# Four output tiles held back behind the last FoX scores, three products on the old weight buffers, and the loads around them moved

## The chip, the core and the metric

The kernel runs on one core of a Trainium2 chip. The metric is the device time of one execution in microseconds (us), as the median of several runs. A profiled execution has its own time, and inside it the span from the first to the last instruction that the profiler recorded. The engines are TensorE (PE in the profile, its weight loads PEld), VectorE (DVE), ScalarE (ACT), GpSimd (POOL) and SyncE (SP), which here only issues transfers: it takes them strictly in program order, and a transfer that waits for a semaphore holds back all that stand behind it.

## What is computed

One step of a decoder layer, for 512 prompt positions and for 8 samples of 8 new positions each (64 rows), 576 columns in all. The attention has a FoX group and a DSA group of 8 heads each; the output projection `w_out` joins them:

```
h = x + concat([fox, dsa]) @ w_out          # w_out rows 0..1023 belong to FoX
f, new_g = conv_ffn(rms_norm(h, g_ffn), prev_g, w_gate, w_up, conv_w, conv_b, w_down)
y = h + f

# FoX of a sample: 1024 cached keys (8 pages of 128) and 8 new ones, 8 heads
s = einsum('bqhd,bkhd->bhqk', q, k) * scale + c_q - c_k
o = einsum('bhqk,bkhd->bqhd', softmax(s), v)
```

## The kernel before

All matrix products are made in three passes of a value split into a high and a low part (high by high, high by low, low by high), with the output features on the partitions and the columns (tokens) along the free axis in two halves of 288 (`HALF`). A product of 1024 inputs by 128 outputs on one half is 24 matmuls, called a product here.

The program is written through a scheduling layer: helper functions record instructions, and the layer sets the order on each engine from its own estimate of when they can start. "Lanes" are generators that `gemm` steps after every second input tile through `pump`; the rate of a lane says how many of its steps one such call takes.

The place of the change is the end of the attention. The output projection has 16 tiles (o = 0 to 15) of 128 output features. Its half 0 is done first, while the samples' FoX attention runs in two lanes beside it: `sa` (scores) and `sb` (values). A sample reads its 8 key pages and 8 value pages (512 KB each) from the cache; TensorE turns the keys (L1413), ACT and DVE split them (L196, L199), TensorE makes the scores (L1434, L1435), DVE and ACT make the softmax (L751 to L782), TensorE turns the weights (L1462) and multiplies them with the values (L1477), and `turned` (L1492, L1494) puts the result into `osum[0]`.

- `w_out_a` makes tiles 5 to 15 (and the DSA rows of tiles 0 to 4 earlier), `w_out_late` (L1369) the FoX rows of tiles 0 to 4 on half 0, for which only prompt columns are needed. Their weights come through `load_w` (L147, buffers `wraw`, `wh`, `wl`) one tile ahead; their sums of squares collect in `ssum0`, which `inverse_rms` (L1524 to L1530) turns into `yn0` with a short chain of small DVE instructions, called the Newton chain here.
- Half 1 of the FoX rows needs the samples, so it comes last: `stage` loads the prompt columns from `odr` (L1297), `fill` and `fill_sample` split them into `gxs`, and a loop over the 16 tiles loads weights (`load_wo`, L1634, buffers `wr`, `wu`, `wl`), multiplies, adds to the rows of h that `load_h` (L1590) brought back, and stores them (L1721). All of these transfers stand in SP's one queue.
- `taps` (L1697, L1698) turns the convolution weights, which SP loads at L1618 and L1619. `half0` normalizes half 0 of h within the same loop.
- Then the gate, up and down products of the MLP follow and fill the rest of the span.

Buffers of later pools lie on memory of earlier ones: the tile `x12`, into which `load_h` brings half 1 of h for tiles 0 to 7, lies where the pool `sx` had, among others, `ob`, `ptile`, `sq0` and the scratch tiles `ms`, `n4_y`, `n4_t` of the Newton chain; `wr0` to `wr3` lie where the key tiles `kraw` were.

Of the kernel before, what the change touches and what calls it, by code (L numbers as in the profile page):

```python
# [49 lines left out]
NLATE = 5  # L50
CTS = (3, 4, 4, 4, 3, 3)
# [4 lines left out]
def tile_hymba_step(  # L56
# [1340 lines left out]

    def fox_scores(b, keep):
# [18 lines left out]
        for w in range(2):  # L1417
# [11 lines left out]
            for h in range(HA):  # L1429
# [5 lines left out]
                T.matmul(sps, qz[:, h * P:(h + 1) * P], kl, start=False, stop=h == 7)  # L1435
# [96 lines left out]
    lane("sa", 2.068)  # L1532
    lane("sb", 1.7)
# [6 lines left out]
    w_out_a(range(NLATE, KD))  # L1540
    for o in range(NLATE):
        w_out_late(o)
# [4 lines left out]
    gxs = fill(fslots, 0, stage(old_x, 0, HALF, TP))  # L1547
# [15 lines left out]
    wp_ctx.close()  # L1563
# [8 lines left out]
    x2_ctx, x2 = opened("x2")  # L1572
    wq_ctx, wq = opened("wq")
    fn_ctx, fn = opened("fn")
    wb_ctx, wb = opened("wb")
# [70 lines left out]

    def multiply(acc, rows, start):


        for k, (wh, wl, xh, xl) in enumerate(rows):  # L1650
            T.matmul(acc, wh, xh, start=start and k == 0, stop=False, skip_group_check=not start)  # L1651
            T.matmul(acc, wh, xl, start=False, stop=False, skip_group_check=not start)  # L1652
        for k, (wh, wl, xh, xl) in enumerate(rows):
            T.matmul(acc, wl, xh, start=False, stop=k == len(rows) - 1, skip_group_check=not start)  # L1654
# [564 lines left out]
```

## Time and profile before

| | us |
|---|---|
| median of 3 runs | 2797.47 |
| lowest and highest | 2793.05, 2798.58 |
| the profiled execution, its own time | 2795.66 |
| its span in the profile | 2793.9 |

The profiled execution is 1.81 us under the median; outside its span lie 1.8 us. In the rows further down, a time is counted from the start of the span. A row of the timeline gives the start, how long it took, engine, line, operation, operands and count, and in brackets how long the engine was idle before and what ended that. The matmuls of TensorE overlap, so that the cost of one is read from start to start, not from its own length.

### The profile page before, as it was taken

Reading aid. Unit: us, or ns where it says so; the run is one execution under the profiler, and the core shown is the slowest. Engines: PE = TensorE matmul, PEld = TensorE weight load, DVE = VectorE, ACT = ScalarE, POOL = GpSimd, SP = SyncE. Lnnn points to the kernel's source line nnn. Section 1 sums busy time; section 2 is a strip of 40 time slices with the busy share of each in tenths; the row PEclk is TensorE's granted clock in tenths of the full one; section 3 lists DMA queues with packets and bytes.
Section 4 is the critical chain, followed back from the end, with each engine's and each line's share of the span. In section 5 each row is a group of like instructions: output and inputs, shape, how many; then the busy total and the mean of one; then the engine's idle time right before and its main releaser. Section 6 shows DMA issues by size and latency. Waiting matters only on the chain.

```text
span 2793.9 us, 53435 instructions
## 1 busy us (share of the span) xinstructions
PE 2709.0 (97%) x20679; PEld 2619.4 (94%) x20679; DVE 2080.8 (74%) x3701; ACT 1346.4 (48%) x2395; POOL 535.5 (19%) x707
## 2 busy tenths in 40 slices
PE   8999999999998999979999999999999999999999
PEld 7998999999898988869999999999999999999999
DVE  6669689555646655547988888888888878888877
ACT  6446644654765444435555454555545543333332
POOL 1333243323554000000012221211111110000000
PEclk9999999999999999989999999999999999999999
DMA  7224343435646699868645554554444476446553
GB/s 212 69 72 108 92 121 90 114 100 160 183 125 216 218 326 308 304 224 241 168 146 159 161 167 150 160 155 135 148 135 145 142 265 218 146 163 210 189 166 111
DMA packets 506776, 469.48 MB, mean 168 GB/s; under 512 B 33360, under 2 KB 451794, under 8 KB 506010
## 3 DMA queue, kind: packets, MB, share of 16 engines
q1 hardware_dynamic: 479481, 363.88, 44.2%
q0 software_dynamic: 26032, 100.12, 9.8%
q8 instruction: 162, 2.65, 0.4%
q10 hardware_dynamic: 1008, 2.06, 0.2%
q14 instruction: 93, 0.75, 0.1%
HBM read 385.37 MB, written 80.36 MB: 167 GB/s over the span
## 4 chain that ended last, share of the span: by engine, by line
PE 61%; DMA 4%; DVE 2%; issue 2%; ACT 1%; SPq 0%; POOL 0%; ACTq 0%; DVEq 0%; POOLq 0%
PE pgemm L1651 10%; PE pgemm L1652 9%; PE pgemm L1654 9%; PE pone L1651 7%; PE pone L1652 7%; PE pone L1654 7%; PE pone L1413 2%; PE pgemm L173 2%; PE pgemm L171 2%; PE pgemm L172 2%; PE pout L1477 1%; PE pq L1434 1%; PE pq L1435 1%; DMA wr<-in_w_down_dram 1%; DVE wl L1644 1%
## 5 line engine op out<-in xcount | busy, mean ns | idle before, releaser
L171 PE MATMUL pgemm<-xh,wh 128*128 128x288 f32 (+1 forms) x1824 | 551.2, 304 | 8.5 <-DVE rawT L1355 3.7
L173 PE MATMUL pgemm<-xh,wl 128*128 128x288 f32 (+1 forms) x1824 | 548.1, 301 | 0.7 <-DVE wl L152 0.7
L172 PE MATMUL pgemm<-xl,wh 128*128 128x288 f32 (+1 forms) x1696 | 509.9, 301 | 3.6 <-DVE xl L300 3.6
L1639 ACT CAST wu<-wr 128x1024 fp32r<-128x1024 f32 (+1 forms) x287 | 292.0, 1019 | 407.5 <-PE pgemm L1652 192.0
L1644 DVE TENSOR_TENSOR wl<-wr,wu 128x1024 fp32r<-128x1024 f32 (+1 forms) x287 | 337.4, 1179 | 37.8 <-ACT wu L1639 33.2
L171 PEld LDWEIGHTS pgemm<-xh,wh 128*128 128x128 f32 (+1 forms) x1824 | 344.9, 189 | 15.1 <-DVE rawT L1355 4.0
L173 PEld LDWEIGHTS pgemm<-xh,wl 128*128 128x128 f32 (+1 forms) x1824 | 345.3, 189 | 5.1 <-DVE wl L152 1.0
L172 PEld LDWEIGHTS pgemm<-xl,wh 128*128 128x128 f32 (+1 forms) x1696 | 321.0, 189 | 7.8 <-DVE xl L300 4.8
L1639 ACT CAST wu<-x 128x1024 fp32r<-128x1024 f32 (+1 forms) x198 | 201.7, 1022 | 258.2 <-PE pgemm L1652 127.5
L1651 PE MATMUL pgemm<-hi,wu 128*128 128x288 f32 x1024 | 280.2, 298 | 4.0 <-DVE ht L2120 3.2
L1651 PE MATMUL pgemm<-xh,wu 128*128 128x288 f32 x992 | 273.0, 301 | 11.3 <-issue 6.7
L1644 DVE TENSOR_TENSOR wl<-x,wu 128x1024 fp32r<-128x1024 f32 (+1 forms) x198 | 233.5, 1183 | 13.1 <-ACT wu L1639 9.0
L1651 PE MATMUL pone<-xh,wu 128*128 128x288 f32 x880 | 240.6, 299 | 2.5 <-ACT wu L1639 2.5
L1652 PE MATMUL pone<-xl,wu 128*128 128x288 f32 x880 | 240.9, 297 | 0.0
L1652 PE MATMUL pgemm<-lo,wu 128*128 128x288 f32 x856 | 232.8, 296 | 0.0
L1652 PE MATMUL pgemm<-xl,wu 128*128 128x288 f32 x824 | 225.2, 297 | 0.0
L1651 PEld LDWEIGHTS pgemm<-xh,wu 128*128 128x128 f32 x992 | 188.1, 190 | 14.9 <-issue 7.6
L1651 PEld LDWEIGHTS pgemm<-hi,wu 128*128 128x128 f32 x1024 | 193.6, 189 | 4.7 <-DVE ht L2120 3.8
L151 ACT CAST wh<-wraw 128x1024 fp32r<-128x1024 f32 (+1 forms) x122 | 127.3, 1045 | 113.6 <-PE pgemm L172 94.5
L152 POOL TENSOR_TENSOR wl<-wraw,wh 128x1024 fp32r<-128x1024 f32 (+1 forms) x51 | 122.0, 2392 | 287.5 <-ACT wh L151 279.2
L1799 POOL DMA_DIRECT2D opd<-pp x140 | 75.7, 542 | 525.8 <-DVE pp L199 501.7
L1651 PEld LDWEIGHTS pone<-xh,wu 128*128 128x128 f32 x880 | 166.5, 190 | 2.6 <-ACT wu L1639 2.6
(556 smaller groups left out, 6639.7 us busy)
## 6 DMA issues: line engine op xcount, KB each, us to landing
wraw<-in_w_in_dram SPq DMA_DIRECT2D x88, 512.0 KB
wr<-in_w_gate_dram SPq DMA_DIRECT2D x85, 512.0 KB
opd<-pp POOLq DMA_DIRECT2D x140, 288.0 KB, 4.0
wr<-in_w_up_dram SPq DMA_DIRECT2D x69, 512.0 KB
kraw<-in_cache_fox_k_dram SPq DMA_DIRECT2D x64, 512.0 KB
vraw<-in_cache_fox_v_dram SPq DMA_DIRECT2D x62, 512.0 KB
wr<-in_w_down_dram SPq DMA_DIRECT2D x38, 512.0 KB
wraw<-in_w_out_dram SPq DMA_DIRECT2D x32, 512.0 KB
```

Source lines behind the costliest of these rows:

```text
L151: A.copy(h[:, :k, :m], raw[:, :k, :m])
L152: (G if share[0] and not u else V).tensor_sub(l[:, :k, :m], raw[:, :k, :m], f(h)[:, :k, :m])
L171: T.matmul(acc[:m, :], h[:, j, :m], xh[:, c], start=kt == 0, stop=False)
L172: T.matmul(acc[:m, :], h[:, j, :m], xl[:, c], start=False, stop=False)
L173: T.matmul(acc[:m, :], l[:, j, :m], xh[:, c], start=False, stop=kt == nk - 1)
L1413: T.transpose(pp[:, g * P:(g + 1) * P], raws[g][:, h * P:(h + 1) * P], ident)
L1639: A.copy(h[:, :n], t[:, :n])
L1644: V.tensor_sub(l[:, :n], t[:, :n], f(h)[:, :n])
L1651: T.matmul(acc, wh, xh, start=start and k == 0, stop=False, skip_group_check=not start)
L1652: T.matmul(acc, wh, xl, start=False, stop=False, skip_group_check=not start)
L1654: T.matmul(acc, wl, xh, start=False, stop=k == len(rows) - 1, skip_group_check=not start)
L1799: (A if n == NP - 1 else G).dma_start(opd[i - 1, n], f(s))
```

## The change

1. Of the five late tiles of half 0 the last four (`HELD`) are made after the lane of the scores has been stepped to its end, and their matmuls may not stand ahead of the last matmul of the scores.
2. The rates of the lanes rise, from 2.068 to 2.25 (scores) and from 1.7 to 1.85 (values).
3. The prompt columns of half 1 are staged earlier and elsewhere: in the second halves of the slots of `xa[0]` in place of the slots of `spare[1]`.
4. The first three products of half 1 (`NEARLY`) take their weights through `load_w` and its buffers, with the jobs that load ahead; `load_h` brings their rows, and the pool `wp` closes after them. The rest of the loop starts at tile 3.
5. The convolution weights are loaded when tile 3 comes, and `taps` stands behind the product of tile 7 in place of tile 3.

```diff
+HELD = 4
+NEARLY = 3
@@
     jobs += [([w_out[:1024, o * P:(o + 1) * P]], 8, P) for o in range(NLATE)]
+    jobs += [([w_out[:1024, o * P:(o + 1) * P]], 8, P) for o in range(NEARLY)]
@@ fox_scores
-                T.matmul(sps, qz[:, h * P:(h + 1) * P], kl, start=False, stop=h == 7)
+                scored[0] = T.matmul(sps, qz[:, h * P:(h + 1) * P], kl, start=False, stop=h == 7).ins
@@
-    lane("sa", 2.068)
-    lane("sb", 1.7)
+    lane("sa", 2.25)
+    lane("sb", 1.85)
@@
     w_out_a(range(NLATE, KD))
+    used = [f(xa[0])[:, k, HALF:] for k in range(8)]
+    gst = stage(lambda: used.pop(0), 0, HALF, TP)
     for o in range(NLATE):
-        w_out_late(o)
+        if o == NLATE - HELD:
+            finish("sa")
+        if o < NLATE - HELD:
+            w_out_late(o)
+        else:
+            with tc.issue_after(scored[0]):
+                w_out_late(o)
     yn0 = const.tile([P, 3], F32, name="yn0")
     inverse_rms(sx, yn0, [ssum0])
     finish("sa", "sb")
     fslots = [t[:, :, :HALF] for t in xa]
-    gxs = fill(fslots, 0, stage(old_x, 0, HALF, TP))
+    gxs = fill(fslots, 0, gst)
@@
-    wp_ctx.close()
@@
+    def fox_out(o, h, l):
+        acc = psum_g() if o % 2 else psum_s()[:, :HALF]
+        outs.append(multiply(acc, [(h[:, k, :], l[:, k, :], *gxs[k]) for k in range(8)], True))
+        V.tensor_add(hh(o, 1), acc, hh(o, 1))
+        S.dma_start(hdr[o, :, HALF:], hh(o, 1))
+
+    load_h(0, 4, 1)
+    for o in range(NEARLY):
+        units = ready.pop(0)
+        prefetch(1)
+        fox_out(o, *units[0])
+    wp_ctx.close()
     x2_ctx, x2 = opened("x2")
     wq_ctx, wq = opened("wq")
@@
-    for i in range(3):
-        S.dma_start(cwr[:, i, :], conv_w[0, i].rearrange("(f p) -> f p", p=P))
-    S.dma_start(cwr[:, 3, :], conv_b[0].rearrange("(f p) -> f p", p=P))
@@ load_wo
-        while len(wos) < min(n, KD):
-            wos.append(wload((0, w_out[:1024, len(wos) * P:(len(wos) + 1) * P])))
+        while len(wos) < min(n, KD - NEARLY):
+            o = NEARLY + len(wos)
+            wos.append(wload((0, w_out[:1024, o * P:(o + 1) * P])))
@@
     load_wo(3)
-    load_h(0, 4, 1)
     load_h(0, 8, 0)
     load_h(8, 16, 0)
     fox0 = half0()
-    for o in range(KD):
-        load_wo(o + 4)
-        if o in (2, 6, 10):
+    for o in range(NEARLY):
+        square(o)
+    for o in range(NEARLY, KD):
+        load_wo(o - NEARLY + 4)
+        if o == 3:
+            for i in range(3):
+                S.dma_start(cwr[:, i, :], conv_w[0, i].rearrange("(f p) -> f p", p=P))
+            S.dma_start(cwr[:, 3, :], conv_b[0].rearrange("(f p) -> f p", p=P))
+        if o == NEARLY:
+            load_h(4, 8, 1)
+        if o in (6, 10):
             load_h(o + 2, o + 6, 1)
-        t = wos[o]
+        t = wos[o - NEARLY]
         h = upper(t, 1024)
         l = lower(t, h, 1024)
-        acc = psum_g() if o % 2 else psum_s()[:, :HALF]
-        multiply(acc, ..., True)
-        V.tensor_add(hh(o, 1), acc, hh(o, 1))
-        S.dma_start(hdr[o, :, HALF:], hh(o, 1))
+        fox_out(o, *[x.rearrange("p (k c) -> p k c", c=P) for x in (h, l)])
         sq1 = square(o)
-        if o == 3:
-            taps()
+        if o == 7:
+            with tc.issue_after(outs[-1]):
+                taps()
```

The layer's order follows. Rows of the changed kernel carry its own line numbers, which are a little higher.

TensorE, from the last score of the last sample (its `pq`) to the first product of half 1, before (`bt` is the softmax, `ptile` its turned weights, `ob` the sample's result):

```order
L1435 MATMUL pq<-ktl,xl 128x512
L1462 MATMUL pone<-ident,bt 128x64 x8
L1465 MATMUL pone<-ident,bt 8x64
L1492 MATMUL pone<-ident,ob 128x128 x2
L1477 MATMUL pout<-vraw,ptile 32x128 x48
L1477 MATMUL pout<-kraw,ptile 32x128 x16
L1477 MATMUL pout<-xl,ptile 32x128 x8
L1492 MATMUL pone<-ident,ob 128x128 x2
L1524 MATMUL pone<-onec,ssum_12431 128x1 x2
L1524 MATMUL pone<-onec,ssum_12431 32x1
L1697 MATMUL pq<-ident,gx 128x43 x4
L1651 MATMUL pone<-xh,wu_16828 128x288
```

The same stretch of the changed kernel, from the values of the last sample on (`pgemm<-xh,wh` at L173 to L175 is a held tile, at L1607 a product of half 1):

```order
L1482 MATMUL pout<-vraw,ptile 32x128 x48
L1482 MATMUL pout<-kraw,ptile 32x128 x16
L1482 MATMUL pout<-xl,ptile 32x128 x8
L173 MATMUL pgemm<-xh,wh 128x288
L174 MATMUL pgemm<-xh,wh 128x288
L175 MATMUL pgemm<-xh,wl 128x288
...
L1497 MATMUL pone<-ident,ob 128x128 x2
L1607 MATMUL pgemm<-xh,wh 128x288
L1529 MATMUL pone<-onec,ssum_12431 128x1 x2
L1529 MATMUL pone<-onec,ssum_12431 32x1
L1607 MATMUL pone<-xh,wh 128x288 x2
L1608 MATMUL pone<-xl,wh 128x288
```

The 96 matmuls of the held tiles stand 64 between the last score and the row that turns `bt`, 23 between that and the values, and 9 behind the values; the convolution weights have left this place, and the sum of squares (L1529) now follows the last held tile directly.

SP's queue at the same place, before, with what each transfer waits for (`DMAHW..` is an earlier transfer on one of eight slots, the others are engines; `xl<-odr` is the staging of half 1, the last two of eight):

```order
L1297 DMA xl_101<-odr_73 128x224 [waits DMAHW2_49,PE_49]
...
L1297 DMA xl_101<-odr_73 128x224 [waits DMAHW1_49]
L1618 DMA gx_16836<-in_conv_w_dram 43x128 [waits DMAHW2_49,Activation_49]
L1618 DMA gx_16836<-in_conv_w_dram 43x128 [waits DMAHW3_49]
L1618 DMA gx_16836<-in_conv_w_dram 43x128 [waits DMAHW4_49]
L1619 DMA gx_16836<-in_conv_b_dram 43x128 [waits DMAHW5_49]
L1634 DMA wr0_16824<-in_w_out_dram 128x8x128 [waits DMAHW6_49]
L1634 DMA wr1_16825<-in_w_out_dram 128x8x128 [waits DMAHW7_49]
L1634 DMA wr2_16826<-in_w_out_dram 128x8x128 [waits DMAHW0_49]
L1590 DMA x12_16816<-hdr_77 128x4x288 [waits DVE_49,DMAHW1_49,PE_49,Activation_49]
L1590 DMA x11_16818<-hdr_77 128x8x288 [waits DMAHW2_49]
```

And in the changed kernel, from the store of the last held tile (`hdr<-x12` are the stores of finished tiles of half 1, `wr` the weights from tile 3 on; the convolution weights are left out):

```order
L1384 DMA hdr_77<-rawT_16714 128x288 [waits DMAHW7_49,DMAHW4_49,DVE_49]
L1600 DMA x12_16809<-hdr_77 128x4x288 [waits DVE_49,DMAHW5_49,PE_49,Activation_49]
...
L1600 DMA x12_16809<-hdr_77 128x4x288 [waits DMAHW2_49]
L1780 DMA stt_17426<-in_state_ffn_conv_dram 128x1x128 [waits DMAHW3_49]
L1620 DMA hdr_77<-x12_16809 128x288 [waits DMAHW5_49,DMAHW4_49,DVE_49]
L1620 DMA hdr_77<-x12_16809 128x288 [waits DVE_49]
L1671 DMA wr0_16924<-in_w_out_dram 128x8x128 [waits DMAHW6_49]
L1671 DMA wr1_16925<-in_w_out_dram 128x8x128 [waits DMAHW7_49]
L1620 DMA hdr_77<-x12_16809 128x288 [waits DMAHW0_49,DVE_49]
```

The weights from tile 3 on have moved behind the stores of tiles 0 and 1 of half 1, and those stand behind the first load of `x12`; the three weights ahead of them come as `wraw` through the old buffers, further up.

VectorE at the end of the sums of squares, before:

```order
L1494 COPY osum_11142<-pone 128x4x8 x4
L199 TENSOR_TENSOR xl<-xl,xh 128x224
L1527 TENSOR_SCALAR ms<-pone 128x2
L1528 TENSOR_SCALAR ms<-pone 32x1
L199 TENSOR_TENSOR xl<-osum_11142,xh 128x8x64
L184 TENSOR_SCALAR n_y<-ms 128x3
L199 TENSOR_TENSOR xl<-xl,xh 128x224 x2
```

And in the changed kernel, from the sum of the last held tile on (`wl<-wraw` is the low part of the weights of tile 2 of half 1):

```order
L1380 TENSOR_TENSOR rawT<-pgemm,rawT 128x288
L1499 COPY osum_11142<-pone 128x4x8 x2
L154 TENSOR_TENSOR wl<-wraw,wh 128x1024
L1522 TENSOR_TENSOR ssum_12431<-ssum_12431,sq_16748 128x288
L201 TENSOR_TENSOR xl<-osum_11142,xh 128x8x64
L1532 TENSOR_SCALAR ms<-pone 128x2
L1533 TENSOR_SCALAR ms<-pone 32x1
L186 TENSOR_SCALAR n_y<-ms 128x3
```

Before, the squares were long done here; now the last tile's sum (L1380), a weight split (L154) and the last square (L1522) stand right ahead of the Newton chain, which begins at L1532.

## Rows read from the trace of the kernel before

**Rows 1.** The page, its head.

```profile
span 2793.9 us, 53435 instructions
```

**Rows 2.** Stretches: us, busy PE PEld DVE ACT POOL, granted clock, DMA share, GB/s.

```profile
1205.00:1235.00 30.00, 23.37 (x342) 18.26 (x340) 11.57 (x27) 9.90 (x20) 0.00 (x0) 0.83 0.52 194
1235.00:1250.00 15.00, 6.60 (x31) 5.99 (x32) 9.00 (x31) 5.56 (x10) 1.35 (x2) 0.66 0.82 240
```

**Rows 3.** Timeline of TensorE, the end of the samples and the first products after.

```profile
1198.63 0.71 PE L1462 MATMUL pone<-ident,bt 64*128 64x64 f32 x8
...
1205.98 1.30 PE L1477 MATMUL pout<-vraw,ptile 128*32 128x128 f32 x40
...
1218.60 0.50 PE L1435 MATMUL pq<-ktl,xl 128*128 128x512 f32 x1
1224.96 1.11 PE L1462 MATMUL pone<-ident,bt 64*128 64x64 f32 x8 [5.86 <-ACT bt L782]
...
1234.09 0.66 PE L1524 MATMUL pone<-onec,ssum 128*128 128x1 f32 x6
1238.36 0.33 PE L1697 MATMUL pq<-ident,gx 43*128 43x43 f32 x1 [3.62 <-DMA gx<-in_conv_w_dram]
...
1244.72 0.61 PE L1651 MATMUL pone<-xh,wu 128*128 128x288 f32 x1 [2.49 <-ACT wu L1639]
...
1249.70 0.29 PE L1651 MATMUL pgemm<-xh,wu 128*128 128x288 f32 x1
...
1252.86 0.29 PE L1651 MATMUL pone<-xh,wu 128*128 128x288 f32 x1
...
1258.96 0.61 PE L1651 MATMUL pgemm<-xh,wu 128*128 128x288 f32 x1 [0.90 <-ACT wu L1639]
...
1263.68 0.29 PE L1651 MATMUL pone<-xh,wu 128*128 128x288 f32 x1
```

**Rows 4.** Timeline of SP's queue: start, time to the last issue's end.

```profile
1212.99 22.32 SPq L1297 DMA_DIRECT2D xl<-odr  x8
1235.40 1.02 SPq L1618 DMA_DIRECT2D gx<-in_conv_w_dram  x3
...
1236.89 4.79 SPq L1634 DMA_DIRECT2D wr<-in_w_out_dram  x3
1241.86 4.16 SPq L1590 DMA_DIRECT2D x<-hdr  x3
1246.06 2.72 SPq L1634 DMA_DIRECT2D wr<-in_w_out_dram  x1
```

**Rows 5.** The values' line L1477: what its idle time waited for, us, times.

```profile
  issue: 11.4, 48
```

**Rows 6.** Timeline of ACT: the splits of the first and fourth weights.

```profile
1243.63 1.04 ACT L1639 CAST wu<-wr 128x1024 fp32r<-128x1024 f32 x1 [1.05 <-DMA wr<-in_w_out_dram]
...
1257.87 1.04 ACT L1639 CAST wu<-wr 128x1024 fp32r<-128x1024 f32 x1 [3.86 <-DMA wr<-in_w_out_dram]
```

**Rows 7.** Timeline of DVE: last late tile, a weight split, the Newton chain.

```profile
1203.07 0.46 DVE L1377 TENSOR_TENSOR rawT<-pgemm,rawT 128x288 f32<-128x288 f32 x1 [1.14 <-PE pgemm L173]
1204.10 0.46 DVE L1517 TENSOR_TENSOR ssum<-ssum,sq 128x288 f32<-128x288 f32 x1 [0.57 <-ACT sq L1516]
...
1238.30 0.15 DVE L185 TENSOR_SCALAR n_y<-n_y 128x3 int32<-128x3 int32 x1
...
1240.87 0.17 DVE L1530 TENSOR_SCALAR yn<-n_y 128x3 f32<-128x3 f32 x1
...
1244.70 1.23 DVE L1644 TENSOR_TENSOR wl<-wr,wu 128x1024 fp32r<-128x1024 f32 x1 [2.99 <-ACT wu L1639]
```

**Rows 8.** Stretches of 10 us as in rows 2, samples and first products.

```profile
1160.00:1170.00 10.00, 10.00 (x130) 8.32 (x130) 4.66 (x9) 3.80 (x7) 0.00 (x0) 1.00 0.56 170
...
1180.00:1190.00 10.00, 10.00 (x72) 9.19 (x71) 7.45 (x12) 6.51 (x12) 0.00 (x0) 1.00 1.03 403
...
1240.00:1250.00 10.00, 5.94 (x29) 5.63 (x30) 5.31 (x16) 3.44 (x4) 0.00 (x0) 0.57 1.03 307
```

More of the change, by code (lines that the diff above doesn't have):

```diff
@@ L1396, in tile_hymba_step @@
     keyed.append(sx)
+    scored = [None]
     def fox_scores(b, keep):
@@ L1570, in opened @@
         return c, c.enter_context(tc.tile_pool(name=name, bufs=1, reuse_waits="tile", **kw))
[L1572 to L1575, printed above, removed]
     hr_ctx, hrp = opened("hr", RIGHT)
@@ L1591, in load_h, with multiply @@
                                              hdr[n0:n1, :, HV[half]].rearrange("k p t -> p k t")))
+    def multiply(acc, rows, start):
+        for k, (wh, wl, xh, xl) in enumerate(rows):
+            T.matmul(acc, wh, xh, start=start and k == 0, stop=False, skip_group_check=not start)
+            T.matmul(acc, wh, xl, start=False, stop=False, skip_group_check=not start)
+        for k, (wh, wl, xh, xl) in enumerate(rows):
+            last = T.matmul(acc, wl, xh, start=False, stop=k == len(rows) - 1, skip_group_check=not start)
+        return last.ins
+    outs = []
+    def fox_out(o, h, l):
[9 more added lines that the diff above has]
+    wp_ctx.close()
+    x2_ctx, x2 = opened("x2")
+    wq_ctx, wq = opened("wq")
+    fn_ctx, fn = opened("fn")
+    wb_ctx, wb = opened("wb")
     wls = [wq.tile([P, 1024], F32R, name=f"wl{i}") for i in range(4)]
@@ L1645, in lower @@
         return l
[L1647 to L1654, printed above, removed]
     def rows8(w, x):
@@ L1710, in tile_hymba_step @@
     fox0 = half0()
-    for o in range(KD):
-        load_wo(o + 4)
-        if o in (2, 6, 10):
+    for o in range(NEARLY):
[9 more added lines that the diff above has]
+        if o in (6, 10):
             load_h(o + 2, o + 6, 1)
-        t = wos[o]
+        t = wos[o - NEARLY]
         h = upper(t, 1024)
         l = lower(t, h, 1024)
-        acc = psum_g() if o % 2 else psum_s()[:, :HALF]
-        multiply(acc, [(h[:, k * P:(k + 1) * P], l[:, k * P:(k + 1) * P], *gxs[k]) for k in range(8)], True)
-        V.tensor_add(hh(o, 1), acc, hh(o, 1))
-        S.dma_start(hdr[o, :, HALF:], hh(o, 1))
+        fox_out(o, *[x.rearrange("p (k c) -> p k c", c=P) for x in (h, l)])
         sq1 = square(o)
-        if o == 3:
-            taps()
+        if o == 7:
+            with tc.issue_after(outs[-1]):
+                taps()
         if o > 3:
```

## The prediction, made before the changed kernel ran

> **What bounds the kernel now.** I read the page first: a span of 2793.9 us [rows 1], almost all of it TensorE's work. So only its idle time and its clock can give time back. I then cut the end of the attention into stretches: in 1205 to 1235 TensorE is busy 23.37 of 30 us, in 1235 to 1250 only 6.60 of 15, with a granted clock of 0.83 and 0.66 [rows 2]. The timeline names the causes [rows 3]. After the last score (1218.60) TensorE waits 5.86 us for the softmax of the last sample. After the sum of squares (1234.09, 0.66 long) it waits 3.62 us for the convolution weights, and 2.49 us more for the first split weights of half 1, whose product starts at 1244.72. The product of tile 0 takes 4.98 us (1244.72 to 1249.70), that of tile 1 3.16 (to 1252.86), that of tile 3 4.72 (1258.96 to 1263.68), and tile 3 starts 2.9 us after tile 2 can have ended: after each of the idle stretches TensorE runs at the 1.2 GHz level for a while, then at 2.4 again.
>
> SP's queue tells why weights come so late: the staging of half 1 holds it from 1212.99 for 22.32 us, and the convolution weights (1235.40) and the first weights (1236.89) stand behind it [rows 4]. The reader is to see that a wait in SP's queue, far from TensorE, sets when half 1 begins.
>
> **The change, step by step.** One product is 24 matmuls in 3.16 us [rows 3], 0.132 each. I call E the end of the last held tile.
>
> *Up to E.* The 96 held matmuls leave the stretch ahead of the last score: 96 x 0.132 = 12.7 us, so the last score moves from 1218.6 to 1205.9. The rates only let the lanes use that room. But the samples now have fewer products between their steps; the values' line has 11.4 us of idle "issue" time over 8 samples [rows 5], 1.4 each, and I add one such share, 1.5 us (bounds 0 and 6, four shares): 1207.4. Then 64 held matmuls take 8.4 us. The softmax needs 6.36 (1218.60 to 1224.96); on ACT a weight split (1.04 [rows 6]) and one square (0.57 [rows 7]) now stand inside it, together 8.0, just covered (bounds 0 and 1). Without this cover the wait would be back at 5.9. Turning `bt` and the previous `ob` costs 1.2 (0.71 for eight of eleven [rows 3]), 23 held matmuls 3.0, the 144 values at 1.30 per 40 [rows 3] 4.7, the last 9 held matmuls 1.2. E = 1207.4 + 18.5 = 1225.9.
>
> *E to the end of tile 2 of half 1.* Here a new wait comes in. Before, the square chain of a late tile ran DVE sum at 1203.07, square, DVE addition at 1204.10, 0.46 long, so 1.5 us in all [rows 7], hidden under other products. Now it is the last tile's, and the orders of ACT and DVE put the weight split of tile 2 into it (1.04 us on ACT ahead of the square [rows 6], 1.23 on DVE ahead of the addition [rows 7]): about 2.9 us until the matmuls of the sum of squares, 0.66 long, may start. `xh` and `xl` of the sample columns come in the same time (bounds 1.7 and 4). The first product starts at E + 3.6, and three take 9.5: E + 13.1.
>
> *SP's queue behind E.* The weights of tile 3 stand behind the stores of tiles 0 and 1, those need `x12`, and `x12` lies on the scratch of the Newton chain. That chain took from 1238.30 to 1241.04 for all but its first three steps [rows 7], 3.3 us with these; from E + 3.7 it ends at E + 7.0. Before, the load of `x12` (1241.86 [rows 4]) also came right behind it, but there only the late weights waited. The smallest convolution load took 2.96 us from issue to its waiter (1235.40 to 1238.36 [rows 3, 4]); `x12` is 0.59 MB, which at 307 GB/s [rows 8] adds 1.9: landed at E + 12.1. Two DVE additions of 0.46, their stores, and the issue of the weights: E + 13.6. Those took 6.7 us before, from 1236.89 to the split at 1243.63 [rows 4, 6], beside other transfers; 2.96 + 1.7 = 4.7 alone. I take 5.5: E + 19.1, and with the split of 1.04 tile 3 starts at E + 20.3 = 1246.2. Before it was 1258.96, so 12.8 us are won here. TensorE will have been idle for some 7 us (bounds: 2.2, since a square of tile 2 and the split come first on ACT, and 13.4, if the weights take the 11.8 us of the fourth one, 1246.06 to 1257.87).
>
> The Trainium skill ("DMA: Bandwidth & Descriptors", Anatomy of one DMA) puts a transfer at a fixed 2.0 us plus its bytes at 436 GB/s, fitted on GpSimd's path; the rows here are slower, 4.7 to 6.7 against an estimated 3.2 by the page. By the page the sum would be 3.5 us lower. The measurement decides.
>
> *Behind tile 3.* Before, the lower clock there cost 4.72 - 3.16 = 1.6 us; after an idle 7 us I expect 1.6 to 3.5, so 1.0 more. The rows of half 0 (2.36 MB) now go out ahead of the weights of tile 6; these may come up to 2 us late, I take 0.9. The taps and a state transpose, 5 of some 0.1, now cost TensorE time between products: 0.5. Their load stands far ahead of them and no longer stops anything; staging half 1 into free slots ends the 22.32 us hold, which is part of the gain above. Together 2.4 given back.
>
> Sum: -12.8 + 2.4 = -10.4. The MLP behind is the same work with weights loaded ahead, and shifts as a whole. The profiled execution (2795.66, its span and 1.8 around it) would come to 2785.3; it lies 1.81 under the median, and from the median the forecast is 2797.47 - 10.4 = 2787.0 us.
>
> **The rivals.**
> *A, the queue behind E is faster than I think.* If the short transfers land at the 2.96 us of the smallest and the Newton chain is not what `x12` waits for, tile 3 waits for the 2.2 us on ACT alone: 5 us less idle and 1 less at the lower clock, 2781. For it: `x12` waits for three engines, and only one of them is the chain. Against it: the two big loads with a waiter took 6.7 and 11.8 us.
> *B, no change that can be measured.* The squeezed samples lose time: four shares of "issue" time in place of one (4.5 us), or the weights of tile 3 wait for 11.8 us instead of 5.5 (6.3 us): 2791.5 to 2793.3, and both 2798. For it: by the order, 79 product matmuls are left in the last full sample where there were 114.
> *C, slower: the cache loads become the bound.* A sample reads 16 x 512 KB = 8.4 MB. From the turning of `bt` at 1198.63 to the last score it was 20.0 us [rows 3], 16 product matmuls (2.1) among them; with the 16 key turns made earlier, about 2, a sample is some 20 us of its own. With 79 product matmuls (10.4) that makes 30.4 us, in which 8.4 MB, three weights, the staged columns and rows of h, 11.9 MB, must come. At the 403 GB/s of the busiest stretch [rows 8] they take 29.5 us, and TensorE never waits. At 307 [rows 8] it would be 38.8, 8.4 late, in each of the last two full samples: 17, with two falls of the clock some 20, so 2807. It decides from 350 GB/s down: 34.0 us, 3.6 late, twice, with the falls the whole gain. Against it: the transfers still have slack stretches (170 GB/s at 1160 to 1170 [rows 8]), and the keys are loaded a window ahead.
> The same skill page ("Where 436 GB/s comes from") holds about 358 GB/s from HBM for one core's binding limit; by that 11.9 MB would take an estimated 33.2 us, 2.8 late per sample, and the forecast would rise to about 2793. The 403 GB/s of [rows 8] disagrees, so I give it little.
> *D, the change does not do what it says:* the held tiles come too late for the wait, because their weights or `rawT` rows are not there. Then 5.9 us are back and the clock falls with them: 2794. All weights but two are issued ahead of the last values, so I count it within B.
>
> **How the numbers follow.** Forecast (2782 to 2791.9) 0.60, A (2777 to 2782) 0.13, B with D 0.19, C 0.08. The range leaves out the lower half of A, the top of B and C: 2780 to 2796; the forecast's own range is 2782 to 2791.9. A change under 0.2% (5.6 us) cannot be told from none here. Faster by more: 0.60 + 0.13 = 0.73; within: 0.19; slower: 0.08.
>
> **What would show it.** In the profile after: the wait of the row that turns `bt` for ACT is gone or under 1 us; one wait of about 2.9 us ahead of the sum of squares; tile 0 of half 1 begins near 1229.5; the load of `x12` is issued about 7 us after the last held tile, and tile 3 waits 5 to 9 us for ACT `wu`, itself for `wr`, near 1246; no wait of TensorE for `kraw` or `vraw` of more than 1 us. I am wrong if TensorE waits for cache loads before 1207, if the wait for `bt` is still there, or if tile 3 follows tile 2 within 3 us.

## The result, and the profile after

The changed kernel takes 2781.82 us (median of 6 runs; 2798.02 before), a ratio of 0.9944 with a 95% interval of 0.9931 to 0.9957. In a second set of runs it is 0.9957 (0.9942 to 0.9973). The profiled execution takes 2779.11 us. The forecast was 2787.0, a ratio of 0.9963 to the median of 2797.47 that it started from.

The stretches that answer to [rows 2] and [rows 8], with the same columns:

```profile
span 2777.3 us, 53435 instructions
1160.00:1180.00 20.00, 20.00 (x213) 17.32 (x206) 11.76 (x22) 8.60 (x17) 0.00 (x0) 1.00 0.91 327
...
1206.00:1225.00 19.00, 19.00 (x256) 17.85 (x254) 8.24 (x17) 7.63 (x13) 0.00 (x0) 1.00 0.39 121
1225.00:1246.00 21.00, 12.43 (x80) 11.77 (x78) 8.50 (x33) 4.14 (x7) 0.00 (x0) 0.83 0.56 156
1246.00:1262.00 16.00, 15.49 (x103) 15.10 (x104) 11.80 (x23) 6.92 (x9) 0.00 (x0) 0.90 1.09 307
```

The timeline of TensorE answers to [rows 3]: the sample before last, the last score, the turning of `bt`, the sum of squares, tiles 0, 1 and 3 of half 1 (the row at 1226.85 is one matmul of tile 1, put ahead of tile 0).

```profile
1185.07 0.50 PE L1440 MATMUL pq<-ktl,xl 128*128 128x512 f32 x1 [0.89 <-DVE sms L783]
1186.32 0.71 PE L1467 MATMUL pone<-ident,bt 64*128 64x64 f32 x8 [0.75 <-ACT bt L784]
...
1206.25 0.50 PE L1440 MATMUL pq<-ktl,xl 128*128 128x512 f32 x1
...
1215.17 0.71 PE L1467 MATMUL pone<-ident,bt 64*128 64x64 f32 x8
...
1224.83 0.38 PE L1497 MATMUL pone<-ident,ob 128*128 128x128 f32 x2
1226.85 0.40 PE L1607 MATMUL pgemm<-xh,wh 128*128 128x288 f32 x1 [1.63 <-ACT xh L198]
1227.71 0.73 PE L1529 MATMUL pone<-onec,ssum 128*128 128x1 f32 x6 [0.47 <-DVE ssum L1522]
1228.37 0.53 PE L1607 MATMUL pone<-xh,wh 128*128 128x288 f32 x2
...
1233.31 0.30 PE L1608 MATMUL pgemm<-xl,wh 128*128 128x288 f32 x1
...
1246.09 0.61 PE L1607 MATMUL pgemm<-xh,wu 128*128 128x288 f32 x1 [6.56 <-ACT wu L1676]
```

The wait for the last sample's `bt` is gone, tile 0 begins at 1228.4, and one new wait of 6.56 us stands ahead of tile 3. Two short ones that the prediction left out, 0.89 and 0.75 us, stand in the sample before last. SP's queue shows where the wait ahead of tile 3 comes from (as [rows 4]):

```profile
1231.84 0.37 SPq L1600 DMA_DIRECT2D x<-hdr  x1
1232.26 1.12 SPq L1745 DMA_DIRECT2D gx<-in_conv_w_dram  x3
1233.42 2.36 SPq L1746 DMA_DIRECT2D gx<-in_conv_b_dram  x1
...
1237.81 0.85 SPq L1620 DMA_DIRECT2D hdr<-x  x2
1238.71 2.06 SPq L1671 DMA_DIRECT2D wr<-in_w_out_dram  x2
```

VectorE and ScalarE, the end of the Newton chain, the addition of tile 0 and the split that tile 3 waits for:

```profile
1231.52 0.17 DVE L1535 TENSOR_SCALAR yn<-n_y 128x3 f32<-128x3 f32 x1
...
1235.88 0.46 DVE L1619 TENSOR_TENSOR x<-pone,x 128x288 f32<-128x288 f32 x1 [3.53 <-DMA x<-hdr]
```

```profile
1244.99 1.04 ACT L1676 CAST wu<-wr 128x1024 fp32r<-128x1024 f32 x1 [4.49 <-DMA wr<-in_w_out_dram]
```

Counted from the last held tile, each row so far stands within some 1 us of where the prediction put it. Two other things do not fit it. The two traces differ ahead of the change already: the same row of the values, the last ahead of the first instruction whose place moved, starts at 984.94 before (first row) and at 980.26 after (second row, of the changed kernel):

```profile
984.94 0.75 PE L1477 MATMUL pout<-vraw,ptile 128*32 128x128 f32 x20
```

```profile
980.26 0.86 PE L1482 MATMUL pout<-vraw,ptile 128*32 128x128 f32 x24
```

I therefore count from matmul 6818 of the record (some 0.6 us behind these rows), called M; up to it the two kernels have the same instructions in the same order. And behind the attention, in the MLP, the kernel before has a wait that the changed one has not, for `cn`, the tile into which small copies gather the columns of `new_g` that TensorE then turns:

```profile
1501.22 0.47 PE L1763 MATMUL pq<-ident,cn 128*126 128x128 f32 x1 [2.77 <-POOL cn L1760]
```

```profile
1491.24 0.27 PE L1797 MATMUL pq<-ident,cn 128*126 128x128 f32 x1
```

The table cuts all traces at the same matmuls (numbers of the record, the last two counted from its end): the last score, tile 3 and matmul 10300 (the first gate products) in us behind M, then the length of two stretches of the MLP. It is worked out from one trace for each kernel.

| kernel | ratio to before (95%) | last score | tile 3 | 10300 | 10300 to 12000 | 17000 to 18200 |
|---|---|---|---|---|---|---|
| before | | 233.1 | 273.4 | 400.5 | 231.4 | 168.8 |
| changed | 0.9944 (0.9931, 0.9957) | 225.4 | 265.2 | 395.6 | 226.8 | 167.6 |
| after_again | 0.9957 (0.9942, 0.9973) | 225.9 | 265.9 | 397.8 | 226.8 | 170.3 |
| e1_no_held | 1.0017 (1.0007, 1.0027) | 234.6 | 268.6 | 397.9 | 230.9 | 178.9 |
| e1b_no_held | 0.9930 (0.9917, 0.9943) | 225.8 | 260.9 | 391.4 | 226.7 | 168.9 |
| e2_no_near | 1.0005 (0.9995, 1.0015) | 226.6 | 269.0 | 404.7 | 230.7 | 167.4 |
| e3_late_stage | 0.9964 (0.9951, 0.9977) | 225.6 | 266.5 | 397.0 | 226.7 | 168.9 |
| b1_held_only | 0.9998 (0.9989, 1.0007) | 225.6 | 269.4 | 397.9 | 226.8 | 177.4 |
| e6_newton | 0.9957 (0.9940, 0.9974) | 226.8 | 263.3 | 393.3 | 227.2 | 168.4 |
| g1_weights_first | 0.9975 (0.9964, 0.9987) | 225.2 | 256.7 | 398.3 | 227.3 | 165.8 |
| g2_weights_first4 | 0.9969 (0.9956, 0.9981) | 223.4 | 254.9 | 390.6 | 231.4 | 167.0 |
| c1_before_cn | 0.9985 (0.9975, 0.9996) | 233.5 | 272.3 | 398.9 | 226.8 | 169.7 |
| h1_free_queue | 0.9937 (0.9923, 0.9950) | 225.0 | 258.1 | 390.1 | 227.3 | 170.3 |
| k1_both | 0.9934 (0.9921, 0.9948) | 224.7 | 253.9 | 385.9 | 227.3 | 168.8 |

The changed kernel's two traces differ by 2.2 us at matmul 10300, and M itself lies between 977 and 990 us in the fourteen. A single difference of under 3 us is therefore not read as an effect.

### The profile page after: what moved, and what is told of

It reads as the page before. It is cut to its first block, busy times and chain, and to the rows that moved or that the text cites. A ratio compares the mean times of both kernels' runs of the same rounds, so it can differ in the third digit from the quotient of the medians.

```text
span 2777.3 us, 53435 instructions
## 1 busy us (share of the span) xinstructions
PE 2707.5 (97%) x20679; PEld 2617.9 (94%) x20679; DVE 2078.2 (75%) x3701; ACT 1344.5 (48%) x2395; POOL 534.5 (19%) x707
## 4 chain that ended last, share of the span: by engine, by line
PE 63%; DMA 2%; DVE 2%; ACT 1%; issue 1%; SPq 0%; POOL 0%; ACTq 0%; DVEq 0%; POOLq 0%
PE pgemm L1607 10%; PE pgemm L1608 10%; PE pgemm L1610 10%; PE pone L1607 7%; PE pone L1608 7%; PE pone L1610 7%; PE pone L1418 2%; PE pgemm L175 2%; PE pgemm L173 2%; PE pgemm L174 2%; PE pout L1482 1%; PE pq L1439 1%; PE pq L1440 1%; DMA wr<-in_w_out_dram 1%; DMA wr<-in_w_down_dram 0%
## 5 line engine op out<-in xcount | busy, mean ns | idle before, releaser
L173 PE MATMUL pgemm<-xh,wh 128*128 128x288 f32 (+1 forms) x1824 | 551.1, 304 | 5.8 <-DVE rawT L1358 1.8
L175 PE MATMUL pgemm<-xh,wl 128*128 128x288 f32 (+1 forms) x1824 | 549.1, 301 | 0.7 <-DVE wl L154 0.7
L173 PEld LDWEIGHTS pgemm<-xh,wh 128*128 128x128 f32 (+1 forms) x1824 | 345.5, 190 | 12.3 <-DVE rawT L1358 2.1
L175 PEld LDWEIGHTS pgemm<-xh,wl 128*128 128x128 f32 (+1 forms) x1824 | 345.7, 190 | 5.2 <-DVE wl L154 1.0
L1607 PE MATMUL pgemm<-xh,wu 128*128 128x288 f32 x984 | 270.7, 300 | 18.4 <-issue 6.7
L1607 PE MATMUL pgemm<-hi,wu 128*128 128x288 f32 x1024 | 279.8, 298 | 4.4 <-DVE ht L2154 3.8
L1607 PE MATMUL pone<-xh,wu 128*128 128x288 f32 x864 | 235.2, 298 | 0.8 <-ACT wu L1676 0.8
L1607 PEld LDWEIGHTS pgemm<-xh,wu 128*128 128x128 f32 x984 | 186.4, 190 | 21.9 <-ACT wu L1676 9.2
L1607 PEld LDWEIGHTS pgemm<-hi,wu 128*128 128x128 f32 x1024 | 193.4, 189 | 5.2 <-DVE ht L2154 4.3
L154 POOL TENSOR_TENSOR wl<-wraw,wh 128x1024 fp32r<-128x1024 f32 (+1 forms) x51 | 122.3, 2397 | 284.2 <-ACT wh L153 269.9
L1610 PE MATMUL pgemm<-hi,wl 128*128 128x288 f32 x1024 | 165.5, 295 | 0.0
```

Source lines behind the costliest of these rows:

```text
L154: (G if share[0] and not u else V).tensor_sub(l[:, :k, :m], raw[:, :k, :m], f(h)[:, :k, :m])
L173: T.matmul(acc[:m, :], h[:, j, :m], xh[:, c], start=kt == 0, stop=False)
L175: T.matmul(acc[:m, :], l[:, j, :m], xh[:, c], start=False, stop=kt == nk - 1)
L1610: last = T.matmul(acc, wl, xh, start=False, stop=k == len(rows) - 1, skip_group_check=not start)
```

## The experiments

**Parts undone, or done alone.** The first undoes changes 1 and 2:

```diff
-HELD = 4
+HELD = 0
-    lane("sa", 2.25)
-    lane("sb", 1.85)
+    lane("sa", 2.068)
+    lane("sb", 1.7)
```

> The changed kernel with no held tile and the old rates (changes 1 and 2 undone, 3 to 5 kept). Theory (one chain): what counts is when tile 3 of half 1 starts, and that hangs on SP's queue behind the samples (load of x12, additions of tiles 0 and 1, their stores, then the weights). The wait for bt (5.9 us) and a lower clock behind it (some 1.6) come back and the squares are early again, so that x12 can come sooner after the values; part of the loss is taken from the 6.56 us of idle time ahead of tile 3. Tile 3 starts 2.5 to 5 us later than in the changed kernel, near 1250; the time is 2785 to 2787. Rival (each cover adds by itself): the whole 7.5 us come back and the wait ahead of tile 3 stays near 6.5; 2789 or more.

The time lies on the rival's side, but for neither reason: the ratio is 0.0060 to 0.0073 above the changed kernel's two, 17 to 20 us. Up to matmul 10300 it is only 0 to 2.3 us behind it, with tile 3 some 3 us later, as the chain has it. The rest is lost in the MLP: 4 us at the wait for `cn` (230.9), and TensorE waits 10.01 us near 2350 (first group below), because VectorE's next instruction waits for a weight load of `w_down` (second group).

```profile
1221.39 1.11 PE L1467 MATMUL pone<-ident,bt 64*128 64x64 f32 x8 [5.36 <-ACT bt L784]
...
1249.60 0.61 PE L1607 MATMUL pgemm<-xh,wu 128*128 128x288 f32 x1 [7.81 <-ACT wu L1676]
...
2360.02 0.61 PE L1607 MATMUL pgemm<-xh,wu 128*128 128x288 f32 x1 [10.01 <-DVE ht L2154]
```

```profile
2358.37 1.23 DVE L1963 TENSOR_TENSOR x<-x,wr 128x1024 f32<-128x1024 f32 x1 [11.82 <-DMA x<-in_w_down_dram]
```

No line there was edited: the layer orders the MLP another way. Three more: `NEARLY = 0`; the staging at its old place and in its old slots; and the kernel before with changes 1 and 2 alone.

```diff
-    used = [f(xa[0])[:, k, HALF:] for k in range(8)]
-    gst = stage(lambda: used.pop(0), 0, HALF, TP)
...
-    gxs = fill(fslots, 0, gst)
+    gxs = fill(fslots, 0, stage(old_x, 0, HALF, TP))
```

> The changed kernel with NEARLY = 0: all sixteen tiles of half 1 take their weights through wr. Theory (one chain): wr0 is issued right behind the load of x12 (near 1232), lands 6.2 us later, and tile 0 starts near 1240 after one idle stretch of some 14 us in place of two of 2.1 and 6.6; tile 3 starts near 1251, with only one stretch at the lower clock: 3 us later than the changed kernel, 2784 to 2786. Rival (the three products only trade one wait for another): tile 3 starts within 1 us of the changed kernel's 1246.1 and the time is the same, 2782. Second rival (each product hides its full length): 9.5 us later, 2791.

The three products are worth more than the 3 us of the theory: 7 to 9 us at matmul 10300, which is nearer to the second rival's 9.5. Tile 3 is 3 to 4 us later, as the theory said; what it left out stands behind. Tile 0 came when expected (1 us sooner against M), but tiles 3 and 4 then wait again, for weights that stand behind the rows of half 0 in the queue:

```profile
1235.41 0.61 PE L1607 MATMUL pone<-xh,wu 128*128 128x288 f32 x1 [10.39 <-ACT wu L1676]
1248.77 0.55 PE L1607 MATMUL pgemm<-xh,wu 128*128 128x288 f32 x1 [2.17 <-ACT wu L1676]
1255.73 0.61 PE L1607 MATMUL pone<-xh,wu 128*128 128x288 f32 x1 [1.99 <-ACT wu L1676]
```

The ratio of 1.0005 is 13 to 17 us above the changed kernel's two; 4 of them are again the wait for `cn` (230.7), which comes with the order of the MLP and not with the products.

> The changed kernel with the staging of half 1 back in the slots of spare[1] and at its old place (change 3 undone alone). Theory (one chain): the staged rows come only behind the last values, the first product of half 1 starts some 4 us later (near 1232.5 in place of 1228.4), the addition of tile 1 and with it the weights of tile 3 move by 2 to 3 us, and tile 3 starts 2 to 4 us later: 2784 to 2786. Rival (absorbed): the later first product is taken whole from the 6.6 us of idle time ahead of tile 3; 2782. Second rival (the 22 us hold of SP was the main cause of the late weights): most of the gain is gone, 2790 or more.

Tile 3 starts 0.6 to 1.3 us later, and the ratio cannot be told from the changed kernel's. The time is the rival's, but nothing had to be absorbed: tile 0 itself begins only some 1 us later against M, where 4 were expected, and the wait ahead of tile 3 is still 6.36 us. The earlier staging is worth little beside the near products, though its hold had looked the longest row of all ([rows 4], 22.32 us).

> The kernel before with changes 1 and 2 alone (four held tiles, higher rates); staging, weights and convolution weights as before. Theory (one chain): the wait for bt goes, but the staging still stands in SP's queue ahead of the convolution weights and the first weights, so that the first product of half 1 starts some 12 us behind the last held tile; 4 to 6 us faster than before, 2792 to 2794. Rival (each cover adds by itself): the full 7.5 us and the held tiles' own share of the queue, 8 us or more: 2790 or less.

Up to matmul 10300 it gains 2.5 us, less than both theories said (4 to 6, and 8): tile 3 starts only 4.0 us sooner. It gains 4.6 more at `cn`, and loses 8.6 between matmuls 17000 and 18200, again at a wait for a load of `w_down`; the time is that of the kernel before.

**The changed kernel again, and the Newton chain.** The second edit is `inverse_rms(const, yn0, [ssum0])`, which puts the scratch tiles elsewhere; the order of transfers and products stays.

> The changed kernel once more, unaltered, for a second profile and a ratio on the chip of the runs beside it. The first two traces differ by 4.7 us already ahead of the first instruction whose order the change touches (matmul 6819 of 20679, near 980 us). If that part is chance, it will vary here by some us, the ratio will lie nearer to the 12 us that lie behind it (0.9957) than to the 16 us of the medians (0.9944), and the stretch from there to the first gate products will again be some 5 us shorter than before, the MLP some 7 us shorter, most of it a wait for cn that is not there. If instead the front is a lasting gain, 0.9944 or less.

The ratio is the one foreseen if the front is chance, but its interval holds 0.9944 too, and the front is 3.9 us shorter again; that it is chance is borne out by all fourteen traces (the last section), not by this run. The stretch from M is 2.6 us shorter than before in this trace, 4.9 in the first. The MLP is not 7 us shorter: the 4.6 us at `cn` are there, but behind matmul 12000 this trace is 4.2 us longer than that of the kernel before, with the same order as the first.

> The changed kernel with the three scratch tiles of the Newton chain in a pool of their own, so that x12 no longer lies on what the chain writes; the order of all transfers and products stays as it is. Theory (one chain): the load of x12 is issued some 3 to 4 us earlier (2.8 in place of 7.0 us behind the last held tile), but the weights of tile 3 then wait for the addition of tile 1, whose product ends 11.6 us behind it; tile 3 starts only 1 to 2 us earlier, and the time is 1 to 2.5 us lower: no difference that can be told. Rival (the Newton chain is the whole of the wait): tile 3 starts 4 us earlier, and with less time at the lower clock the kernel gains 4 to 5.5 us.

`x12` is issued at 1232.48, some 2.8 us behind the last held tile in place of 7.0, and the wait ahead of tile 3 falls from 6.56 to 3.33 us. Tile 3 starts some 2 us sooner against M, as the chain said, and the ratio is that of the second set.

**Weights ahead of the stores.** Both put the stores of tiles 0 to 2 behind the first weights (`last_w`: the last weight load issued), the second also `load_wo(4)` and the second load of `x12` ahead of the rows of half 0:

```diff
     load_wo(3)
+    with tc.issue_after(last_w[0]):
+        for o in range(NEARLY):
+            S.dma_start(hdr[o, :, HALF:], hh(o, 1))
```

> The changed kernel with the Newton scratch apart, and the stores of tiles 0 to 2 of half 1, the convolution weights and the square of tile 2 put behind the first three weights (wr) of tile 3 on. Theory (one chain): the weights are issued some 4 to 5 us behind the last held tile, land before tile 2 is done, tile 3 follows tile 2 within 0.5 us, no fall of the clock: 6.6 + 1.6 us less, some of it given back at tile 6, whose weights still stand behind 2.4 MB of rows: 5 to 8 us faster than the changed kernel. Rival (the transfers get in each other's way): x12 and three weights share the DMA engines, the additions of tiles 0 to 2 come late, and the wait comes back at tile 3 or 4; 2 us or less.

> As the run before, with the fourth weights and the second load of x12 ahead of the 2.4 MB of rows of half 0 as well. Theory (one chain): tile 6 finds its weights too; the whole 8 us up to the MLP. The layer orders the MLP behind in another way than in the changed kernel (as in the runs without near tiles and with late staging), so that up to 3 us may come back at the wait for cn: 5 to 8 us faster than the changed kernel. Rival: as for the run before.

Tile 3 follows tile 2 without a wait in both, 9 to 11 us sooner than in the changed kernel. Of g1 all is given back, at tiles 6 and 7 for the most part (waits of 2.79 and 3.66 us). In g2 the wait moves to tile 7, whose weights stand in SP's queue behind the convolution weights, four transfers of 22 KB that take it 8.3 us to issue:

```profile
1263.24 0.61 PE L1607 MATMUL pgemm<-xh,wu 128*128 128x288 f32 x1 [5.03 <-ACT wu L1681]
```

```profile
1247.44 6.58 SPq L1755 DMA_DIRECT2D gx<-in_conv_w_dram  x3
1254.07 1.72 SPq L1756 DMA_DIRECT2D gx<-in_conv_b_dram  x1
1255.89 4.39 SPq L1674 DMA_DIRECT2D wr<-in_w_out_dram  x3
```

Of the 5 to 7 us that g2 gains up to matmul 10300, 4.6 are lost at the wait for `cn` (231.4). Neither ratio is below the changed kernel's: the rival's side.

**The wait for `cn`, alone.** In the kernel before:

```diff
-        G.tensor_copy(c[:, i * 2:i * 2 + 2], gx[:, TP:TP + 2])
+        copy = A.copy if i == m - 1 else G.tensor_copy
+        copy(c[:, i * 2:i * 2 + 2], gx[:, TP:TP + 2])
```

> The kernel before, with one edit far from the change: in the MLP, the last two of every fourteen small copies into cn go to ACT in place of GpSimd; the order of everything else is the same, word for word. In the traces so far the stretch between matmuls 10300 and 12000 of the record takes 226.7 to 227.3 us in the changed kernel and four others, where the first transpose of cn finds its tile ready, and 230.7 to 231.4 us in the kernel before and three others, where TensorE waits 2.4 to 2.9 us there and then runs at the lower clock for a while. Theory (a part of the change's gain is this wait, which the layer's order brings or leaves out): the stretch takes 227 us here too and the time falls by 3 to 5 us, to a ratio of 0.9985. Rival (the wait is a symptom, other work is late there): the stretch stays above 230 us and the ratio is 1.

As the theory said: 226.8 us and 0.9985. That the ratio agrees to the digit is luck, since its interval runs from 1 to 7 us; but it leaves out no change. So some 4 to 5 us of what the change brought can be had without any of it.

**Combined.** h1 is g2 with the convolution weights on GpSimd's queue (`G.dma_start`) and c1's edit; e1b is e1 with a rate of 2.1; k1 is both.

> The best of what the runs showed, put together: the run with the first four weights ahead of the stores and of the rows of half 0, the convolution weights on GpSimd's queue in place of SP's (there they held back the weights of tile 7, which TensorE waited 5.0 us for), and the copies into cn as in the run beside it. Theory (one chain, and the wait for cn apart): no wait of more than 1 us between the last held tile and the end of half 1 but the one ahead of the sum of squares; the stretch from matmul 6818 to 10300 takes 384 to 387 us (390.6 in the run with four weights first, 395.6 and 397.8 in the changed kernel), the one from 10300 to 12000 takes 227; 8 to 12 us faster than the changed kernel, a ratio of 0.9915 to 0.993 to the kernel before. Rival (each wait that goes is given back at the next transfer): 0.9955 as the changed kernel.

The stretch from M is the shortest but for k1's, though 3 us longer than foreseen, with a wait of 2.25 us left at tile 7; 0.9937 lies between the theories.

> The run without held tiles once more, with a rate of 2.1 in place of 2.068 for the scores: a number that makes the layer order the MLP behind as in the other runs, where the one at 2.068 had a wait of 10.2 us near 2350 for a load of w_down. Theory (the loss of that run was mostly the order behind, not the missing held tiles): the wait near 2350 is 2 us again and that for cn is gone, the time is 12 to 15 us lower than there, near the changed kernel: a ratio of 0.996 to 0.9985. Rival (the held tiles themselves are worth the 20 us): 1.0 or more.

Faster than either theory said. It tests less than its name says: by the layer's order a rate of 2.1 alone leaves 73 matmuls of the late tiles behind the last score, with no tie, and 3 behind the turning of `bt`. There is no wait for `bt`, tile 3 starts 7.7 us sooner than in e1, and 4 to 5 us sooner than in the changed kernel. So it does not tell what late tiles behind the last score are worth, only that they need no tie. The wait near 2350 is 1.86 us, that of VectorE 2.63 (compare 11.82):

```profile
2335.39 1.23 DVE L1963 TENSOR_TENSOR x<-x,wr 128x1024 f32<-128x1024 f32 x1 [2.63 <-DMA x<-in_w_down_dram]
```

> The two best runs together: no held tiles and rates of 2.1 and 1.7 (which leave 73 matmuls of the late tiles behind the last score without a tie, and none behind the values), and the freed queue of the other run (four weights ahead of the stores, convolution weights on GpSimd's queue, Newton scratch apart, copies into cn on ACT). Theory (the gains stand at different places and add): the sum of squares is done some 4 us sooner than with held tiles, tile 3 follows tile 2 without a wait, near 255 us behind matmul 6818 (261 and 258 in the two runs), the stretch from matmul 6818 to 10300 takes 385 to 388 us (391.4 and 390.1), and the ratio to the kernel before is 0.990 to 0.992. Rival (the transfers of half 1 are the bound by now): the wait moves to tiles 6 to 8, the stretch stays at 390 us and the ratio at 0.993 to 0.994.

In the trace the gains add: tile 3 at 253.9, the stretch 385.9 us, 14.6 less than before and 10 to 12 less than the changed kernel. The ratio, 0.9934, is the rival's, and does not show more than that of e1b or h1. It beats the kernel before clearly; below the changed one it lies by some 3 to 6 us, with intervals that overlap, so that this is not shown.

## Why the prediction was right, and where not

The time lies in the range and on the forecast side, but in good part by luck. At 2781.82 it lies just under the forecast's own range (2782 to 2791.9), where rival A stood, and A's mechanism did not come: tile 3 waited 6.56 us, not some 2. The medians are 12 to 16 us apart where 10.4 were forecast; what the traces show of it comes only in part from where the prediction put it.

*What held: the chain from E to tile 3.* The last held tile ends at 1224.8, and from there on: the first product at E + 3.6, measured 3.5 (1228.37); the Newton chain's end at E + 7.0, measured 6.9; `x12` landed at E + 12.1 (its own terms give 11.9), measured 11.1; the weights' issue at E + 13.6, measured 13.9; tile 3 at E + 20.3, measured 21.3, after 6.56 us idle (7 foreseen). From issue to their waiter, the load of `x12` took 4.0 us and that of the weights 6.3. By the Trainium skill ("DMA: Bandwidth & Descriptors", Anatomy of one DMA), whose fit is for GpSimd's path, they would take an estimated 3.4 and 3.2; the trace, of SP's queue, does not agree, and the measurement decides. (Against the prediction's own terms that is 1.5 and 2.3 less, 3.8 together, not the 3.5 that it gives.) Rival C did not come: TensorE waits once for `kraw`, 0.39 us at 995.8, and is never idle between 1160 and 1180, at 327 GB/s.

*What was mis-sized: the squeezed samples.* The term was 1.5 us (bounds 0 and 6). 12.7 us of matmuls left the stretch, and the last score moved by 7.2 to 7.7 us against M: the samples cost 5.0 to 5.5, near the upper bound. The source of the term was misread: the 11.4 us of [rows 5] are all idle time of the weight loads (PEld), and the matmuls of that line never stood idle. The cost is elsewhere. TensorE, which before had no wait between M and the last score, now has 2.0 us (2.5 in the second trace), most of it in the rows at 1185 and 1186; behind these two its clock falls for a while, which takes another 1.7 us (the first row below; [rows 8] has 1.00 there). Some 1.3 us are in no single wait. In the sample before last, the low part of a key split (`ktl`) stands behind a weight split on VectorE (the row at 1185.07 names the instruction after it, `sms`; in the second trace the same row names `ktl`), and the softmax behind two weight splits and a key split on ScalarE. So the wait for `bt` was not only removed, a part moved one sample ahead:

```profile
1185.00:1195.00 10.00, 9.18 (x100) 6.39 (x100) 4.54 (x13) 5.73 (x14) 1.33 (x2) 0.83 0.89 259
```

```profile
1183.18 1.23 DVE L154 TENSOR_TENSOR wl<-wraw,wh 128x1024 fp32r<-128x1024 f32 x1 [0.49 <-ACT wh L153]
1184.33 0.69 DVE L201 TENSOR_TENSOR ktl<-pone,kth 128x512 fp32r<-128x512 f32 x1
```

```profile
1182.10 1.05 ACT L153 CAST wh<-wraw 128x1024 fp32r<-128x1024 f32 x1 [1.28 <-PE pgemm L174]
1183.05 0.58 ACT L198 CAST kth<-pone 128x512 fp32r<-128x512 f32 x1
1183.53 1.16 ACT L782 ACTIVATE bt<-bt,fnm 64x1032 f32<-64x1032 f32 x1
```

E (1225.9 foreseen) and tile 3 (1246.2, measured 1246.09) hit the forecast only because the whole trace was 4.7 us early at M. Against M, E comes 3.6 us late, and tile 3 gains 7.5 to 8.2 us, not 12.8. The lower clock also fell on tile 0 (4.94 us, 1228.37 to 1233.31), which I had left out; it is hidden by the wait ahead of tile 3.

*Behind tile 3* 2.4 us were to be given back; it is 3.3 and 4.9. Of these the lower clock on tile 3 was to be 1.6 to 3.5 (no row gave the 3.5); the product takes 4.7 and 5.8 us, so 1.5 and 2.6 over the 3.16. So up to matmul 10300 the change gains 4.9 and 2.6 us, not 10.4.

*The step that failed: "The MLP behind is the same work with weights loaded ahead, and shifts as a whole."* It does not: an edit ahead of it can make the layer order it another way. Between matmuls 12000 and 17000 TensorE's instructions stand in just two orders in the fourteen traces: that of the kernel before (with e1, e2, g2, c1, h1 and k1) and that of the changed one (with e1b, e3, b1, e6 and g1). With the first order the stretch from 10300 to 12000 takes 230.7 to 231.4 us, unless the last copies into `cn` are on ScalarE (c1, h1, k1: 226.8 to 227.3); with the second it takes 226.7 to 227.3. Likewise e1 and b1 alone have five loads of `w_down` at another place in SP's queue, and they alone take 177 to 179 us between 17000 and 18200, the others 166 to 170.

So between matmuls 10300 and 12000 the changed kernel is 4.6 us shorter, and c1 shows that the wait for `cn` is the cause. Before, GpSimd's copies into `cn` take 3.12 and 1.95 us, while VectorE runs sums of two SBUF operands back to back; after, 1.61 and 0.19, the second in a gap of VectorE (timelines below, the kernel before first). TensorE asks for the tile 2.3 us after the copies began before, and 2.4 after: their length decides. Before, it waits 2.77 us, and the lower clock behind the wait (third group, as [rows 2]: 0.66 granted in these 5 us) takes 1.7 more.

```profile
1496.14 1.22 DVE L1644 TENSOR_TENSOR wl<-x,wu 128x1024 fp32r<-128x1024 f32 x1
1496.15 3.12 POOL L1759 COPY cn<-gx 128x2 f32<-128x2 f32 x1 [2.36 <-DVE gx L1773]
1497.27 1.22 DVE L1931 TENSOR_TENSOR wr<-x,wr 128x1024 f32<-128x1024 f32 x1
...
1499.21 1.95 POOL L1760 COPY cn<-gx 128x16 f32<-128x16 f32 x1
```

```profile
1488.80 1.61 POOL L1793 COPY cn<-gx 128x2 f32<-128x2 f32 x1 [2.38 <-DVE gx L1807]
...
1490.35 0.19 POOL L1794 COPY cn<-gx 128x16 f32<-128x16 f32 x1
...
1491.22 0.46 DVE L201 TENSOR_TENSOR pp<-tb,pp 128x288 fp32r<-128x288 f32 x1 [0.85 <-ACT pp L198]
```

```profile
1501.00:1506.00 5.00, 4.78 (x25) 4.78 (x26) 4.04 (x7) 2.05 (x4) 1.20 (x3) 0.66 0.46 133
```

The Trainium skill ("GPSIMD Engine Reference", Key points) says that GpSimd shares its SBUF interfaces with VectorE and contends with instructions of two SBUF inputs; these rows agree. That the contention alone makes 3.12 of 1.61 us was not isolated; that the wait is worth 4.6 us was, by c1. That the other place of the `w_down` loads makes the waits of e1 and b1 goes with all fourteen traces, but no run moved these loads alone.

*The sum.* Of the 12 to 16 us of the medians, 2.6 to 4.9 lie between M and the first gate products and 4.6 at `cn`. The other 3 to 9 us are in no stretch that both traces of the changed kernel share, and stay open: behind matmul 12000 the first is 2.4 us shorter than before, the second 4.2 longer, and with one trace a run the 13 us by which M varies cover them.

*My second theory fared no better.* "One chain up to tile 3" foresaw when tile 3 starts (e1, e2, e6, g1, g2; not e3), but not the time: behind tile 3 the same queue is late again (e2, g1, g2), until the weights of tiles 6 and 7 stand free too (h1, k1, with 2.25 and 1.56 us left at tile 7).

## What to carry to other kernels

Where a layer orders instructions from its own estimates, an edit can change the order of much that follows: cut both traces at the same matmuls and compare the stretches before a total is put down to the edit. A wait removed from a shared queue came back here at the next transfers behind it, so look at the queue until its waiters have slack, not at the first waiter. Idle time in a view is to be asked for by engine before it is priced: that of the weight loads cost the matmuls nothing here. Cover for a wait can be had by a tie or by a rate; here the rate (e1b) was cheaper in the trace: the sum of squares starts 242.3 us behind M, with the tied tiles 246.9, where a split and the last tile's square stand ahead of it.

## What was not expected of the hardware

The same copy of 128x2 elements took 0.78 to 3.11 us on GpSimd (36 times) and 0.19 on ScalarE (7 times), in c1:

```profile
L1760 POOL COPY cn<-gx x36: 776/1242/3114, 1373.1 to 2219.6; 128x2 f32<-128x2 f32 x36
...
L1760 ACT COPY cn<-gx x7: 186/192/194, 1491.6 to 2269.0; 128x2 f32<-128x2 f32 x7
```

Identical instructions in identical order (in eight of the traces, on every engine) reached M after 977 to 986 us; with four more that differ by the place of one memset it is up to 990. Whole executions of one kernel differ by some 10 to 16 us, so a large part of the spread can arise in the first third of the span.

Part of it is the clock. Ahead of matmul 5870 TensorE waits for the same tile in every trace. After a wait of the same 1.53 us its clock fell in e6 and did not in the second trace of the changed kernel (e6 first in both groups, the granted clock is the third number from the end). Of the fourteen traces it fell there in five, whose stretch from matmul 5000 to 6000 took 150.7 to 153.8 us, and not in nine, with 147.2 to 150.5:

```profile
843.19 0.38 PE L1207 MATMUL pout<-dsvl,dpt 128*128 128x256 f32 x1 [1.53 <-POOL dsvl L201]
...
842.18 0.39 PE L1207 MATMUL pout<-dsvl,dpt 128*128 128x256 f32 x1 [1.53 <-POOL dsvl L201]
```

```profile
843.00:853.00 10.00, 9.57 (x41) 8.30 (x42) 1.67 (x3) 2.15 (x5) 4.18 (x3) 0.66 0.20 56
...
842.00:852.00 10.00, 9.58 (x64) 8.47 (x65) 3.52 (x6) 3.58 (x7) 4.18 (x3) 1.00 0.33 83
```
